# Weight halves of an MLP made by two Pool DMAs each, one casting and one adding

## The chip, the cores and the metric

The kernel runs on one core of one Trainium2 chip. The metric is the device time of one execution in microseconds (us); lower is better.

## The reference

The reference is one layer of a decoder trunk over 256 tokens of width 2048: RMSNorm, one combined projection into three attention mixers, three branch projections merged by sigmoid gates, an output projection with residual, and then the part that matters here, the MLP:

```python
h = rms_norm(x, norm_mlp[layer])
x = x + jnp.square(jax.nn.relu(h @ w_mlp_in[layer])) @ w_mlp_out[layer]
return rms_norm(x, norm_final)
```

`w_mlp_in` is 2048 x 8192 and `w_mlp_out` 8192 x 2048, both float32. The two are 134.2 MB together, and each weight is used once per execution.

## The kernel before, in words

Every dense product is done in three passes of a rounded format (`float32r`, F32R): a float32 number is split into a high part `hi` and a low part `lo = w - hi`, and the products hi x hi, hi x lo and lo x hi are summed in PSUM.

All dense work is one list, `steps`. A step is 512 KB of weights (128 partitions x 1024 numbers) and the matmuls that use them. For one step three things happen before TensorE can start: `load` (L67 to L70) fetches the raw weights with a DMA issued on SP, `fetch` (L72 to L81) makes `hi` as a copy with a change of type on ScalarE (L79) and `lo` as a subtraction on VectorE (L80). The tiles lie in the pool `ring`, with three tags (`raw`, `hi`, `lo`) of four buffers each.

The order of instructions on every engine is the order in which the code writes them (`manual_schedule`, L44). The last loop (L883 to L896) goes through the steps: it emits the preparation of a step (`pre`), one piece of the attention or transposition tasks (`advance`), what follows the step before (`post`, the emptying of PSUM), then `fetch` of the step `AHEAD` = 3 later, then the matmuls of the step itself.

The MLP is the last 256 steps. `mlp_in(p)` makes up to four groups of 256 hidden columns; each group is four steps of `dmajor` (weights stationary, L224 to L228; rows of 256 numbers). Its result is emptied by `half` (L690), `hu` (L691, L692) and `hid` (L693, L694). `mlp_out(p)` is up to sixteen steps of `tmajor` (activations stationary, L251 to L253; rows of 512 numbers), and its result is added to `acc` (L704). The order is `mlp_in(0)`, then `mlp_in(p)` and `mlp_out(p - 1)` in turn, and at the end `mlp_last`, whose four steps (L720 to L722) do the first token tile, then the second one from the same weights, then the last norm.

The Pool queue carries few things: small constants at the start, `spread_rows` (L195) and `load_master` (L203) for the attention bias, two memsets (L540), `load_nf` (L764, the gains of the last norm) and some arithmetic of the last norm. None of the weights go through it.

Of the kernel before, what the change touches and what calls it, by code (L numbers as in the profile page):

```python
# [8 lines left out]
F32 = mybir.dt.float32  # L9
F32R = mybir.dt.float32r  # L10
AF = mybir.ActivationFunctionType
OP = mybir.AluOpType
# [10 lines left out]
NB = 383  # L23
AHEAD = 3

# column offsets in w_in
AQ, AKC, AVC, AKS, AVS, AKW, AVW = 0, 1024, 1280, 1536, 1792, 2048, 2304
BQ, BK, BV = 2584, 3608, 3864
CQ, CK, CV = 4120, 5144, 5400
# [4 lines left out]
def hybrid_block(ctx: ExitStack, tc: tile.TileContext, x, w_in, cmp_pos, cmp_w1, cmp_w2, swa_sinks,  # L34
                 w_branch, w_out, w_mlp_in, w_mlp_out, norm_mix, norm_mlp, norm_final, rel_bias,
                 onehot, rmask, cmask, out):
    nc = tc.nc
    big = ctx.enter_context(tc.tile_pool(name="big", bufs=6))
    ring = ctx.enter_context(tc.tile_pool(name="ring", bufs=4))
# [15 lines left out]
    def pair(name="pair"):  # L55
        return psum.tile([128, 2, 512], F32, name=name, tag="mm")

    # ---------------------------------------------------------------- streamed weights
    steps = []
    tasks = []  # L60

    def add(src, a, b, mm, pre=None, post=None):
        steps.append((src, a, b, mm, pre, post))
# [3 lines left out]
    def load(j):  # L67
        src, a, b = steps[j][:3]
        loaded[j] = ring.tile([128, a, b], F32, name="raw", tag="raw")
        nc.sync.dma_start(loaded[j], src)  # L70

    def fetch(j):  # L72
        if j not in loaded:
            load(j)
        raw = loaded.pop(j)
        a, b = steps[j][1:3]
        hi = ring.tile([128, a, b], F32R, name="hi", tag="hi")
        lo = ring.tile([128, a, b], F32R, name="lo", tag="lo")
        nc.scalar.activation(hi, raw, AF.Copy)  # L79
        nc.vector.tensor_tensor(lo, raw, hi.bitcast(F32), op=OP.subtract)  # L80
        return hi, lo  # L81
# [10 lines left out]
        while any(t[0] == name for t in tasks):  # L92
            advance()

    # ---------------------------------------------------------------- constants
    xt = bigt([128, 2, D], F32, "xt")

    def load_x(c0, c1):
# [29 lines left out]
    hm = cst.tile([128, 4], F32, name="hm")  # L128
    nc.vector.tensor_reduce(hm, ident.rearrange("p (h c) -> p h c", h=4), axis=AX.X, op=OP.add)

    # ---------------------------------------------------------------- first norm
    part = cst.tile([128, 2, 4], F32, name="part")
    rs = cst.tile([128, 2], F32, name="rs")
    rsh = cst.tile([128, 2], F32, name="rsh")
# [2 lines left out]
    HT = [bigt([128, 8, 512], F32R, f"HT{i}") for i in range(2)]  # L137

    def split_scaled(tiles, k, src, g0):
        """hi and lo parts of two K tiles, src * gain, into columns 0:256 and 256:512."""  # L140
        d = [tiles[(k + a) // 8][:, (k + a) % 8] for a in range(2)]
        g = [gains[:, g0 + k + a:g0 + k + a + 1] for a in range(2)]
        for a in range(2):
            nc.scalar.activation(d[a][:, 0:256], src[:, a], AF.Copy, scale=g[a])
        for a in range(2):
            nc.vector.scalar_tensor_tensor(d[a][:, 256:512], src[:, a], g[a], d[a][:, 0:256].bitcast(F32),
                                           op0=OP.mult, op1=OP.subtract)
# [4 lines left out]
        nc.vector.tensor_copy(gains[:, c0:c0 + n], pc[:, 0:n])  # L152

    def x_block(i):
        """Two K tiles of x * gain; the row factor of the norm follows where products leave PSUM."""
        b = bank("xT").rearrange("p (a q) -> p a q", a=2)
        for a in range(2):
            k = 2 * i + a
            for tt in range(2):
                nc.tensor.transpose(b[:, a, tt * 128:(tt + 1) * 128], xt[:, tt, k * 128:(k + 1) * 128], ident)  # L160
        split_scaled(HT, 2 * i, b, 0)
# [29 lines left out]
        yield  # L191

    def spread_rows(m):
        """Row h 128 times at pitch 384; read at pitch 383 it is a Toeplitz matrix."""
        nc.gpsimd.dma_start(scr[m * 8:(m + 1) * 8, :, 0:NB],  # L195
                            rm[m * 8:(m + 1) * 8, None, :].to_broadcast([8, 128, NB]))

# [6 lines left out]
                                       ap=[[383, 128], [128 * 384, 4], [1, 256]]))  # L204
        masters[m, g] = t

    # ---------------------------------------------------------------- dense jobs
    def dmajor(w, c0, rhs, evac, kts=KT, pre=None, cuts=(0, 4, 8, 12, 16)):
        """256 columns of w as [column, token]: weights stationary."""
        st = {}  # L210
        for k0, k1 in zip(cuts, cuts[1:]):
            src = w[k0 * 128:k1 * 128, c0:c0 + 256].rearrange("(k p) c -> p k c", p=128)

            def mm(hi, lo, k0=k0, k1=k1):
                if k0 == 0:
                    st["ps"] = pair()
                ps = st["ps"]
                for k in range(k1 - k0):
                    kt = k0 + k
                    r = rhs(kt)  # L220
                    for c in range(2):
                        cs = slice(c * 128, (c + 1) * 128)
                        if kt:
                            nc.tensor.matmul(ps[:, c, 0:256], lo[:, k, cs], r[:, 0:256],  # L224
                                             start=False, stop=False)
                        nc.tensor.matmul(ps[:, c, :], hi[:, k, cs], r, start=kt == 0, stop=kt == kts - 1)  # L226
                        if not kt:
                            nc.tensor.matmul(ps[:, c, 0:256], lo[:, k, cs], r[:, 0:256],  # L228
                                             start=False, stop=False)

            add(src, k1 - k0, 256, mm, pre if k0 == 0 else None,
                (lambda: evac(st["ps"])) if k1 == kts else None)

    def tmajor(w, c0, n, lhs, evac, kts=KT, kc=2, pre=None):
        """n columns of w as [token, column]: activations stationary."""
        st = {}
        for k0 in range(0, kts, kc):
            src = w[k0 * 128:(k0 + kc) * 128, c0:c0 + n].rearrange("(k p) c -> p k c", p=128)

            def mm(hi, lo, k0=k0):  # L240
                if k0 == 0:
                    st["ps"] = pair()
                ps = st["ps"]
                for k in range(kc):
                    kt = k0 + k
                    l = lhs(kt)
                    for tt in range(2):
                        o = ps[:, tt, 0:n]
                        lh = l[:, tt * 128:(tt + 1) * 128]
                        ll = l[:, 256 + tt * 128:256 + (tt + 1) * 128]  # L250
                        nc.tensor.matmul(o, lh, hi[:, k], start=kt == 0, stop=False)  # L251
                        nc.tensor.matmul(o, lh, lo[:, k], start=False, stop=False)  # L252
                        nc.tensor.matmul(o, ll, hi[:, k], start=False, stop=kt == kts - 1)  # L253

            add(src, kc, n, mm, pre if k0 == 0 else None,
                (lambda: evac(st["ps"])) if k0 + kc == kts else None)
# [19 lines left out]
        for tt in range(2):  # L276
            nc.scalar.activation(dst[:, tt], ps[:, tt, c0:c0 + n], func, scale=scale[:, tt:tt + 1])

    # ---------------------------------------------------------------- projections
    w = w_in[0]  # L280
    qT, kT, vt = {}, {}, {}

# [36 lines left out]
            tasks.append(("A", attn_a(1)))  # L319
        tmajor(w, AVW, 280, hT, ev, kc=2)  # L320

    # ---------------------------------------------------------------- compression of blocks
    XH = {}
    kcT = cst.tile([128, 30], F32, name="kcT")
    vcr = cst.tile([128, 2, 128], F32, name="vcr")
# [86 lines left out]
            nc.vector.tensor_copy(vcr, pk[:, 0:256].rearrange("p (g d) -> p g d", g=2))  # L412
        yield

    # ---------------------------------------------------------------- attention
    oT = {}

    def new_o(m):
# [1 line left out]
            oT[m] = bigt([128, 8, 512], F32R, "oT")  # L420

    def core(m, g, q, k, v, o, first, last, gate):
        """Causal attention of the four heads of one kv group; o accumulates [d, (head, token)]."""
        M = masters[m, g]
        h0 = 4 * g
        qp = att.tile([128, 2, 4, 128], F32R, name="qp", tag="P0")
# [9 lines left out]
        for i in range(2):  # L436
            b = bank("s1").rearrange("p (h k) -> p h k", h=2)
# [143 lines left out]
        store_o(0, g, o)  # L581
        yield

    # ---------------------------------------------------------------- gates and branches
    gt = {}

    def gates(m):
# [26 lines left out]
            tmajor(w_branch[0, m], c * 512, 512, lambda kt: oT[m][:, kt], ev, kts=8, pre=pre)  # L614

    def to_dmajor(src, c, dst, gain0):
        """Column chunk c of a [token, column] tile, transposed and split into hi and lo parts."""
        if not dst:
            dst += [bigt([128, 8, 512], F32R, "dmaj") for _ in range(2)]
        for i in range(2):  # L620
# [12 lines left out]
                split_scaled(dst, k, b, gain0)  # L633
            yield

    # ---------------------------------------------------------------- output projection
    acc = {}
    H2 = []

# [34 lines left out]
        nc.vector.reciprocal(r2, r2)  # L674
        yield

    # ---------------------------------------------------------------- MLP
    hid = {}

    parts = [(4 * i, 4) for i in range(7)] + [(28, 3), (31, 1)]  # L680
# [27 lines left out]
    fin = {}  # L708

    def mlp_last(p):  # L710
        """The last K tiles: the first token tile is done before the second, from the same weights."""
        keep = []
        r0 = parts[p][0] * 256

# [68 lines left out]
            nc.scalar.dma_start(rows[:, 1280:2048], o[:, 1280:2048])  # L783
            nc.sync.dma_start(rows[:, 640:1280], o[:, 640:1280])

    # ---------------------------------------------------------------- order of the work
    def job(f, *a, **kw):
        """The steps of one dense job, taken off the list."""
        n = len(steps)
        f(*a, **kw)  # L790
        r = steps[n:]
        del steps[n:]
        return r
# [29 lines left out]
    n = len(steps)  # L823
# [28 lines left out]
    n = len(steps)  # L852
    out_proj()
    steps[n + 6] = before(steps[n + 6], lambda: drain("M"))
    n = len(steps)
    mlp_in(0)
    steps[n + 3] = before(steps[n + 3], lambda: drain("H"))
    for p in range(1, len(parts)):
# [3 lines left out]
    mlp_last(len(parts) - 1)  # L862
    steps[n - 4] = before(steps[n - 4], load_nf)

    # ---------------------------------------------------------------- emission
    ready = {}
    load_x(0, 256)
    load(0)
# [17 lines left out]
    for j in range(len(steps)):  # L886
        _, _, _, mm, pre, post = steps[j]
        if pre:
            pre()
        advance()  # L890
        if late:
            late()
        if j + AHEAD < len(steps):
            ready[j + AHEAD] = fetch(j + AHEAD)
        mm(*ready.pop(j))
        late = post  # L896

# [3 lines left out]


def _constants():
    """Distance buckets and causal masks of the two token tiles: they follow from the shapes alone."""
    import math
    import numpy as np
    dist = 255 - np.arange(NB)
# [28 lines left out]
```

## Time and profile before

| | |
|---|---|
| median of 2 runs | 1610.4 us (1610.1 to 1610.7) |
| profiled execution, span | 1610.1 us |
| TensorE busy | 1534.5 us, 95% |
| VectorE busy | 940.4 us, 58% |
| ScalarE busy | 718.8 us, 45% |
| Pool busy | 23.9 us, 1% |
| read from HBM | 290.02 MB |

The span is the time from the first to the last instruction of one profiled execution. Busy shares are means over stages that differ. The MLP is the stretch from about 889 us to the end, and what a change to it does is read there.

### The profile page before, as it was taken

The numbers are of one execution on the slowest core, as the hardware profiler recorded it, in microseconds if no ns is written. First come the engines' busy times: TensorE is split into PE (matmuls) and PEld (weight loads), VectorE is DVE, ScalarE is ACT, GpSimd is POOL, SyncE is SP. The second block draws the span as 40 slices with busy tenths as digits, with TensorE's granted clock in tenths as the row PEclk, the third lists the DMA queues.
The fourth block names the chain that finished last, engine by engine and source line by source line (L and its number), as shares of the span: only waits on it lengthen the run. The fifth ranks groups of instructions, "written<-read, shape, count | busy, mean of one in ns | idle before, by whom it ended". The sixth has DMA issues, their size and how long they took to land.

```text
span 1610.1 us, 20195 instructions
## 1 busy us (share of the span) xinstructions
PE 1534.5 (95%) x7878; PEld 1305.1 (81%) x7878; DVE 940.4 (58%) x1082; ACT 718.8 (45%) x942; POOL 23.9 (1%) x33
## 2 busy tenths in 40 slices
PE   8995997899959999999999999999999999999997
PEld 7894885688849888888888888888888888888885
DVE  5772663565637547744755666565655566555656
ACT  6551542455524445444445444343434444443443
POOL 1000000000000000000000000000000000000002
PEclk9997999899979999999999999999999999999999
DMA  8696756655666665566655656656565656566563
GB/s 248 193 276 110 223 158 126 174 169 173 176 138 172 183 194 187 168 183 192 225 187 184 188 177 197 192 190 190 186 195 188 193 181 198 181 198 194 189 218 118
DMA packets 211231, 298.16 MB, mean 185 GB/s; under 512 B 10268, under 2 KB 129612, under 8 KB 210752
## 3 DMA queue, kind: packets, MB, share of 16 engines
q1 hardware_dynamic: 207504, 287.15, 58.2%
q0 software_dynamic: 3456, 9.33, 3.8%
q8 instruction: 61, 1.00, 0.3%
q10 hardware_dynamic: 176, 0.40, 0.1%
q14 instruction: 34, 0.28, 0.1%
HBM read 290.02 MB, written 6.80 MB: 184 GB/s over the span
## 4 chain that ended last, share of the span: by engine, by line
PE 90%; DMA 7%; DVE 1%; issue 1%; ACT 1%; POOL 0%; POOLq 0%; DVEq 0%; ACTq 0%
PE pair L226 22%; PE pair L251 17%; PE pair L253 17%; PE pair L252 17%; PE pair L224 11%; DMA raw<-in_w_in_dram 5%; DMA raw<-in_w_branch_dram 2%; PE s L440 1%; PE obank L509 1%; PE pair L228 1%; DVE lo L80 1%; ACT hi L79 1%; PE tm L625 0%; PE obank L512 0%; PE cps L362 0%
## 5 line engine op out<-in xcount | busy, mean ns | idle before, releaser
L80 DVE TENSOR_TENSOR lo<-raw,hi 128x1024 fp32r<-128x1024 f32 (+2 forms) x542 | 653.5, 1213 | 540.1 <-ACT hi L79 538.9
L79 ACT ACTIVATE hi<-raw 128x1024 fp32r<-128x1024 f32 (+2 forms) x542 | 564.3, 1048 | 668.7 <-PE pair L253 385.5
L226 PE MATMUL pair<-dmaj,hi 128*128 128x512 f32 x1024 | 359.8, 398 | 0.0
L224 PE MATMUL pair<-dmaj,lo 128*128 128x256 f32 x960 | 269.7, 281 | 0.0
L226 PEld LDWEIGHTS pair<-dmaj,hi 128*128 128x128 f32 x1024 | 190.8, 188 | 44.5
L226 PE MATMUL pair<-HT,hi 128*128 128x512 f32 x576 | 206.8, 401 | 0.0
L251 PE MATMUL pair<-hi,hid 128*128 128x512 f32 x496 | 192.9, 389 | 0.0
L252 PE MATMUL pair<-lo,hid 128*128 128x512 f32 x496 | 192.9, 389 | 0.0
L253 PE MATMUL pair<-hi,hid 128*128 128x512 f32 x496 | 192.9, 389 | 0.0
L251 PE MATMUL pair<-hi,HT 128*128 128x512 f32 (+2 forms) x512 | 190.0, 371 | 2.7 <-ACT hi L79 2.7
L252 PE MATMUL pair<-lo,HT 128*128 128x512 f32 (+2 forms) x512 | 187.6, 366 | 0.4 <-DVE lo L80 0.4
L253 PE MATMUL pair<-hi,HT 128*128 128x512 f32 (+2 forms) x512 | 187.6, 366 | 0.0
L224 PEld LDWEIGHTS pair<-dmaj,lo 128*128 128x128 f32 x960 | 181.3, 189 | 1.4
L224 PE MATMUL pair<-HT,lo 128*128 128x256 f32 x540 | 153.1, 284 | 2.0 <-DVE lo L80 2.0
L226 PEld LDWEIGHTS pair<-HT,hi 128*128 128x128 f32 x576 | 109.4, 191 | 23.8 <-PE obank L576 0.2
L251 PEld LDWEIGHTS pair<-hi,HT 128*128 128x128 f32 x512 | 98.0, 191 | 17.6 <-ACT hi L79 3.0
L252 PEld LDWEIGHTS pair<-lo,HT 128*128 128x128 f32 x512 | 98.1, 192 | 15.3 <-DVE lo L80 0.6
L253 PEld LDWEIGHTS pair<-hi,HT 128*128 128x128 f32 x512 | 98.0, 191 | 15.3
L252 PEld LDWEIGHTS pair<-lo,hid 128*128 128x128 f32 x496 | 93.1, 188 | 19.4
L253 PEld LDWEIGHTS pair<-hi,hid 128*128 128x128 f32 x496 | 93.1, 188 | 19.4
L251 PEld LDWEIGHTS pair<-hi,hid 128*128 128x128 f32 x496 | 93.1, 188 | 18.9
L224 PEld LDWEIGHTS pair<-HT,lo 128*128 128x128 f32 x540 | 103.0, 191 | 3.1 <-DVE lo L80 2.2
(211 smaller groups left out, 1354.2 us busy)
## 6 DMA issues: line engine op xcount, KB each, us to landing
raw<-in_w_in_dram SPq DMA_DIRECT2D x178, 512.0 KB, 3.8
raw<-in_w_mlp_in_dram SPq DMA_DIRECT2D x128, 512.0 KB, 3.9
raw<-in_w_mlp_out_dram SPq DMA_DIRECT2D x128, 512.0 KB, 4.4
raw<-in_w_branch_dram SPq DMA_DIRECT2D x48, 512.0 KB, 4.4
raw<-in_w_out_dram SPq DMA_DIRECT2D x32, 512.0 KB, 4.4
raw<-in_cmp_w_dram SPq DMA_DIRECT2D x16, 512.0 KB, 4.6
scr<-rm POOLq DMA_DIRECT2D x3, 1532.0 KB, 36.1
master<-scr POOLq DMA_DIRECT2D x6, 512.0 KB, 5.2
```

What stands on the lines that cost most here:

```text
L79: nc.scalar.activation(hi, raw, AF.Copy)
L80: nc.vector.tensor_tensor(lo, raw, hi.bitcast(F32), op=OP.subtract)
L224: nc.tensor.matmul(ps[:, c, 0:256], lo[:, k, cs], r[:, 0:256], start=False, stop=False)
L226: nc.tensor.matmul(ps[:, c, :], hi[:, k, cs], r, start=kt == 0, stop=kt == kts - 1)
L228: nc.tensor.matmul(ps[:, c, 0:256], lo[:, k, cs], r[:, 0:256], start=False, stop=False)
L251: nc.tensor.matmul(o, lh, hi[:, k], start=kt == 0, stop=False)
L252: nc.tensor.matmul(o, lh, lo[:, k], start=False, stop=False)
L253: nc.tensor.matmul(o, ll, hi[:, k], start=False, stop=kt == kts - 1)
L440: nc.tensor.matmul(b[:, h], qp[:, a, 2 * i + h], kp[:, c], start=n == 0, stop=n == 2)
L509: nc.tensor.matmul(ob, v[:, a, 0, g * 128:(g + 1) * 128], P0[c][:, hs], start=first and n == 0, stop=False, skip_group_check=True)
```

## The change

For the steps of the MLP alone (index `from_dma[0]` and up) `fetch` no longer loads raw weights. One DMA on the Pool queue reads the weights into `hi`, a tile of type F32R; ScalarE writes `lo = -hi`; a second DMA on the Pool queue reads the same weights again and adds them onto `lo`. The twelve buffers of the ring are shared out so that each step takes two of them and six steps fit. The steps of the MLP are fetched five ahead in place of three. (The rest of the diff removes comments.)

```diff
+    from_dma = [1 << 30]
...
+    def fetch_by_dma(j):
+
+        src, a, b = steps[j][:3]
+        tags = ("raw", "hi", "lo")
+        hi = ring.tile([128, a, b], F32R, name="hi", tag=tags[2 * j % 3])
+        lo = ring.tile([128, a, b], F32R, name="lo", tag=tags[(2 * j + 1) % 3])
+        nc.gpsimd.dma_start(hi, src)
+        nc.scalar.activation(lo, hi.bitcast(F32), AF.Copy, scale=-1.0)
+        nc.gpsimd.dma_start(lo, src, accum_op=OP.add)
+        return hi, lo
+
     def fetch(j):
+        if j >= from_dma[0]:
+            return fetch_by_dma(j)
         if j not in loaded:
             load(j)
...
     n = len(steps)
+    from_dma[0] = n
     mlp_in(0)
...
-        if j + AHEAD < len(steps):
-            ready[j + AHEAD] = fetch(j + AHEAD)
+        for i in range(j + 1, min(j + (AHEAD if j < from_dma[0] else AHEAD + 2), len(steps) - 1) + 1):
+            if i not in ready:
+                ready[i] = fetch(i)
         mm(*ready.pop(j))
```

## Rows read from the trace of the kernel before

**Rows 1.** The page, busy time (us, share, instructions) and granted clock by slices.
```profile
PE 1534.5 (95%) x7878; PEld 1305.1 (81%) x7878; DVE 940.4 (58%) x1082; ACT 718.8 (45%) x942; POOL 23.9 (1%) x33
...
PEclk9997999899979999999999999999999999999999
```

**Rows 2.** Busy time by windows: stretch, length, engines, PEclk, DMA share, GB/s.
```profile
905.00:1560.00 655.00, 655.00 (x3327) 556.63 (x3326) 388.28 (x386) 282.30 (x300) 0.55 (x1) 1.00 0.61 191
```

**Rows 3.** The chain that ended last, MLP: start us, us, what.
```profile
1034.72 0.46 PE pair L226 x2
...
1123.39 0.46 PE pair L226 x2
```

**Rows 4.** Groups by line and form in 905:1560: busy us, mean ns, idle before.
```profile
L80 DVE TENSOR_TENSOR lo<-raw,hi 128x1024 fp32r<-128x1024 f32 x237 | 287.4, 1224 | 197.8 <-ACT hi L79 197.8
L79 ACT ACTIVATE hi<-raw 128x1024 fp32r<-128x1024 f32 x238 | 248.4, 1056 | 271.8 <-PE pair L253 162.2 <-PE pair L226 78.8 <-ACT hi L79 22.7
```

**Rows 5.** The page, DMA issues: count, KB each, median us to landing.
```profile
raw<-in_w_mlp_in_dram SPq DMA_DIRECT2D x128, 512.0 KB, 3.9
raw<-in_w_mlp_out_dram SPq DMA_DIRECT2D x128, 512.0 KB, 4.4
```

**Rows 6.** The timeline of POOL: start us, us, instruction, idle before.
```profile
163.37 0.78 POOL L203 DMA_DIRECT2D master<-scr  x1 [34.21 <-DMA raw<-in_w_in_dram]
164.14 0.33 POOL L540 MEMSET Lc<- 128x256 f32 x1
252.15 0.76 POOL L203 DMA_DIRECT2D master<-scr  x1 [87.67 <-DVE L L450]
...
1544.68 0.55 POOL L764 DMA_DIRECT2D nf<-in_norm_final_dram  x1 [924.56 <-DMA raw<-in_w_mlp_out_dram]
```

**Rows 7.** The timeline of PE around the wait of Rows 6.
```profile
157.30 1.03 PE L378 MATMUL cT<-fold,cs 60*128 60x30 f32 x4 [17.89 <-DVE cs L372]
```

**Rows 8.** The timeline of DVE ahead of the second `master` DMA.
```profile
251.17 0.68 DVE L450 SCALAR_TENSOR_TENSOR L<-s,master 128x512 f32<-128x512 f32 x1
251.77 1.21 DVE L454 TENSOR_REDUCE nm<-L 128x4 f32<-128x1024 f32 x1
```

**Rows 9.** The line L203: its Pool DMAs of 512 KB, us to landing.
```profile
DMA to landing us min/median/max: 4.2/5.2/6.4
```

**Rows 10.** The line L70 in 905:1560: SP's loads of 512 KB, us to landing.
```profile
DMA to landing us min/median/max: 3.4/4.0/5.9
```

**Rows 11.** DMA queues in 905:1560: packets, MB, share of 16 engines.
```profile
q1 hardware_dynamic: 94146, 123.75, 60.0%
```

**Rows 12.** DMA queues and issues in 128:164, where `scr` is written from Pool.
```profile
q0 software_dynamic: 704, 1.57, 43.1%
...
scr<-rm POOLq DMA_DIRECT2D x1, 1532.0 KB, 35.1
```

**Rows 13.** DMA queues and issues in 1544:1552, where `nf` is loaded.
```profile
q0 software_dynamic: 144, 1.05, 33.5%
...
nf<-in_norm_final_dram POOLq DMA_DIRECT2D x1, 1024.0 KB, 7.0
```

**Rows 14.** Busy time by windows (as Rows 2): the busiest DMA stretch, and two idle ones.
```profile
10.00:15.00 5.00, 5.00 (x29) 4.51 (x28) 2.34 (x5) 1.98 (x4) 0.00 (x0) 1.00 1.06 353
...
140.00:146.00 6.00, 0.00 (x0) 0.00 (x0) 0.00 (x0) 0.00 (x0) 0.00 (x0) 0.62 0.60 83
146.00:152.00 6.00, 0.00 (x0) 0.00 (x0) 0.00 (x0) 0.00 (x0) 0.00 (x0) 0.50 0.51 61
```

**Rows 15.** The timeline at the edges of the MLP, and the last step group.
```profile
873.52 27.78 SPq L70 DMA_DIRECT2D raw<-in_w_mlp_in_dram  x11
...
889.15 0.39 PE L226 MATMUL pair<-dmaj,hi 128*128 128x512 f32 x1
...
1588.15 0.39 PE L720 MATMUL pair<-hi,hid 128*128 128x512 f32 x1
```

## The prediction

> **What bounds the kernel now.** I read the page first: TensorE is busy 95% of the span, and its granted clock is low only in slices of the first third [rows 1]. Then the windows: from 905 to 1560 us, nearly the whole MLP, TensorE is busy 655.00 of 655.00 us at a granted clock of 1.00, and the DMA engines are at 0.61 with 191 GB/s [rows 2]. The chain of waits says the same: in the MLP it names only matmuls, and repeats after 1123.39 - 1034.72 = 88.67 us for 32 steps, **2.77 us a step** [rows 3]. The groups by line show the split: 1.06 us of ScalarE and 1.22 us of VectorE a step, both waiting for others [rows 4]. So nothing that the change removes ends anything last in this stage. What it puts in must stay below 2.77 us a step, or it becomes the bound.
>
> **What is removed.** 256 loads on SP [rows 5], 256 subtractions (256 x 1.22 = 313 us of VectorE) and 256 copies on ScalarE, which come back as 256 negations of the same size, 1.06 us [rows 4]. All of it lay beside the matmuls: worth nothing.
>
> **What is added: 512 DMAs on Pool, in a chain.** Pool's order per step is: DMA into hi, then DMA onto lo. The second waits for the negation, the negation for the landing of hi; and behind the waiting lo DMA stands the hi DMA of the next step. Does Pool hold what stands behind? At 163.37 it issues a DMA for which it had waited, and a memset follows at 164.14 [rows 6]. The memset's buffer had last been read by matmuls that end at 158.33 [rows 7], so it could have run some 5 us earlier: it was held. Fetching five steps ahead doesn't help, since the chain links each step to the next: hi(j), negation(j), lo(j), hi(j+1). One link costs:
>
> - From the end of the negation to lo's issue: 0.3 us, as from the end of the VectorE operation before L454 (251.85) to Pool's DMA at 252.15 [rows 6, 8]. Landing to negation isn't shown by itself; I count it in the landing.
> - Issue of lo: 0.76 us, as the Pool DMA of 512 KB in rows of 1 KB [rows 6]; 0.55 us, as for nf, at the low end [rows 6].
> - hi(j+1) from issue to landing: 4.2 us, the shortest of the six `master` DMAs of the same size [rows 9]. I take the shortest because the other traffic of the stage (SP's loads) is gone; the longest, 6.4, is the high end. The cast, which no row shows, is in this spread.
> - hi(j+1) behind lo(j): the two follow each other through the same 16 engines, hi's issue 0.76 us later. A plain load of 512 KB keeps all 16 busy 0.600 x 655 / 236 = 1.67 us (123.75 MB are 236 loads) [rows 11]. The add must also read what is there, twice the reads: I take 3.34 us, an estimate, so hi waits 3.34 - 0.76 = 2.58 us. Low end 0 (the two overlap; less is excluded, as lo's transfer can't speed hi's). High end: the one Pool write that was slow, 43.1% of 36 us = 15.5 us for 1.57 MB, so 5.2 us per 512 KB [rows 12], a wait of 4.44 us. I stay nearest to the plain row, since the weights' rows are long and contiguous.
> - The negation: 1.06 us [rows 4].
>
> The sum is 0.3 + 0.76 + 4.2 + 2.58 + 1.06 = **8.9 us a step**, against 2.77. Low end: 0.3 + 0.55 + 4.2 + 0 + 1.06 = 6.1. High end: 0.3 + 0.76 + 6.4 + 4.44 + 1.06 = 13.0.
>
> The doubled reads have a parallel in the Trainium skill ("Collectives: The Full Stack", section "The bandwidth ceiling: the fold count and why AG ≠ RS ≠ AR"): the DMA's add emits two reads per chunk, and the collective that adds moves half as much per second as the one that copies. No row here shows an adding DMA.
>
> **What hides under the chain.** TensorE's step takes 2.77 us, and 5.5 us if its clock falls to half, which rows with TensorE idle show: 0.50 from 146 to 152 us [rows 14]. Both are below 6.1, so TensorE only waits. PSUM is emptied behind the negation of a step four later on ScalarE's queue, but the matmuls that need that bank also need lo of that step, which comes after the same negation: no extra wait. half, hu and hid (some 2.7 us, once in four steps) then sit ahead of the next negation, in the time in which its hi is still on the way (4.2 us or more). If hi landed at once this cover would be gone, and they would cost up to 2.7 us in each of 32 groups, 86 us. nf (1.05 MB) moves past Pool's weight DMAs near the end: 0.55 us of issue and 33.5% of 8 us = 2.7 us of engines [rows 13], some 3 us. The ring's buffers bind nothing: hi(j+6) needs step j done.
>
> **The sum.** The first hi DMA can leave between SP's first MLP load now, 873.5, and about 881, three steps before the MLP's first matmul at 889.15 [rows 15]: 878. lo of that step is issued 4.2 + 1.06 + 0.3 later, at 883.6; lo of the last step 255 links later, 883.6 + 255 x 8.9 = 3153. It lands after 4.2 + 1.67 = 5.9. After the last step's weights come its matmuls and the last norm. Now these take from 1588.15 + 3 x 1.36 = 1592.2 to 1610.1 = 17.9 us [rows 15]; 30 matmuls of 0.227 us at half clock add 6.8. With nf: 3153 + 5.9 + 24.7 + 3 = 3187, **3190 us**. The profiled execution (1610.1) and the median (1610.4) are the same here. Ends: 883.6 + 255 x 6.1 + 4.2 + 17.9 = 2460; 883.6 + 255 x 13.0 + 8 + 27.7 = 4230.
>
> **Rivals.**
>
> - *Pool doesn't hold hi(j+1)*, steps overlap, and the DMA engines bind: 1.67 + 3.34 = 5.0 us a step, 878 + 256 x 5.0 + 30 = 2190 us; with an add as cheap as a copy 3.34, 1765 us. For it: twelve buffers and five steps of look-ahead. Against: the held memset. 0.07.
> - *Short DMAs*: hi lands in 3.4 us, the shortest of SP's loads [rows 10], and isn't delayed by lo: 0.3 + 0.55 + 3.4 + 1.06 = 5.3, 883.6 + 255 x 5.3 + 3.4 + 17.9 = 2256 us. Against: none of six Pool DMAs landed below 4.2. 0.04. The Trainium skill ("DMA: Bandwidth & Descriptors", section "Anatomy of one DMA — SWDGE (gpsimd) path") has a rule for this: about 2.0 us plus the bytes at 436 GB/s, 3.2 us for 512 KB; with that the link would be 0.3 + 0.76 + 3.2 + 0.44 + 1.06 = 5.8 and the time about 2385. By that rule, the trace doesn't agree: its Pool DMAs took 1.0 to 3.2 us longer [rows 9].
> - *The add is far slower* than any row: four times the scr rate, 20.8 us, a link of 26 us and some 7600 us. For it: no row shows an add. 0.04.
> - *Not slower*: both DMAs of every step are done within 2.77 us and TensorE stays without gaps, so 1610 us. That needs 1.05 MB in 2.77 us = 379 GB/s with nothing for the add's second read; the best 5 us here are 353, with the engines full [rows 14]. It decides only if the chain doesn't. 0.015. Faster by over 2% is 32 us, and the stage has no idle TensorE time to give: 0.005.
> - *The change doesn't do what it says*: if the DMA into hi copied the bits without rounding, lo would come out zero; the same DMAs and waits remain, and so the time.
>
> **How the numbers follow.** The serial chain between 6.1 and 13.0 us a link has 0.83; the rivals take the rest. The range, 2460 to 4230, is that case alone and leaves out 0.17. A measurement of this kernel can tell about 2% from no change. Slower by over 2%: 0.98; within: 0.015; faster: 0.005.
>
> **What would show it.** Right: Pool's waits split between ScalarE (negation) and nothing else; the chain of waits in the MLP made of DMA hi, ACT, POOL; the MLP's DMA issue rows showing hi at 4 to 7 us to landing and the start of consecutive lo issues 8.9 us apart; granted clock near 0.5; TensorE's idle time put down to the DMA onto lo. HBM reads up by 134 MB to about 424 MB. Wrong: hi issues of several steps in a row with no lo between (Pool passes), a gap between lo issues under 6 or over 13 us, or DMA share near 1 (the engines bind, not the chain). The term I trust least is the add: if hi's landing is much beyond 4.2 + 2.6 us, that is the one that was mis-sized.

## The result, and the profile after

The changed kernel takes **3233.6 us** (3232.3 to 3234.8, 2 runs) against 1610.4: a ratio of 2.008, 95% interval 2.004 to 2.012. The forecast was 3190 us in a range of 2460 to 4230. The profiled execution has a span of 3230.5 us, and its terms are taken against that.

The page after: busy time, and by slices of 1/40 of the span TensorE's busy tenths, its granted clock and the share of the DMA engines; then the Pool queue's packets and the memory traffic.

```profile
PE 2100.9 (65%) x7878; PEld 1666.3 (52%) x7878; DVE 631.2 (20%) x826; ACT 721.3 (22%) x942; POOL 527.0 (16%) x545
...
PE   9797989999955555555555555555555555555554
...
PEclk9898989999966766666666667666666666666776
DMA  7766566666566655565566556555655655555555
...
q0 software_dynamic: 208256, 277.80, 44.2%
...
HBM read 424.24 MB, written 6.80 MB: 133 GB/s over the span
```

The first eleven slices, to 888 us, are the part ahead of the MLP's matmuls, which the change doesn't touch; from the MLP on, TensorE is busy half the time. The memory is read for 134 MB more, the second read of the MLP's weights. And yet the DMA engines' share is no higher than before (0.59 here against 0.61 [rows 2]), and no engine is full. That points to latencies that follow one another. The windows of the MLP (length, PE, PEld, DVE, ACT, POOL busy, granted clock, DMA share, GB/s) say the same:

```profile
905.00:3180.00 2275.00, 1249.06 (x3505) 944.18 (x3505) 112.98 (x167) 301.29 (x318) 492.23 (x501) 0.69 0.59 116
```

The waits of the whole execution (engine and line, what it waited for, us in total, times, longest):

```profile
POOL lo L81 <- ACT lo L80: 1779.2, 250, 8.9
...
ACT lo L80 <- DMA hi<-in_w_mlp_out_dram: 987.0, 128, 10.4
ACT lo L80 <- DMA hi<-in_w_mlp_in_dram: 984.7, 128, 8.8
...
PEld pair L266 <- DMA lo<-in_w_mlp_out_dram: 556.4, 123, 6.2
PE pair L266 <- DMA lo<-in_w_mlp_out_dram: 491.9, 123, 5.8
```

Pool waits for the negation, the negation for hi's landing, TensorE for lo's. That is the chain of the prediction, read from the waits. The page's own chain of waits doesn't show it: it has 59% under "issue", time for which it found no releaser, so it can't serve as the evidence here.

The start of the MLP shows the chain link by link. The timeline of ScalarE and Pool (start us, us, instruction, idle before and its releaser; the other engines' rows are left out):

```profile
877.63 0.75 POOL L79 DMA_DIRECT2D hi<-in_w_mlp_in_dram  x1 [261.16 <-PE pair L267]
...
881.89 1.06 ACT L80 ACTIVATE lo<-hi 128x1024 fp32r<-128x1024 f32 x1 [5.95 <-DMA hi<-in_w_mlp_in_dram]
...
883.25 1.33 POOL L81 DMA_DIRECT2D lo<-in_w_mlp_in_dram  x1 [4.88 <-ACT lo L80]
...
884.04 1.32 POOL L79 DMA_DIRECT2D hi<-in_w_mlp_in_dram  x1
...
891.12 1.06 ACT L80 ACTIVATE lo<-hi 128x1024 fp32r<-128x1024 f32 x1 [8.17 <-DMA hi<-in_w_mlp_in_dram]
...
892.48 1.27 POOL L81 DMA_DIRECT2D lo<-in_w_mlp_in_dram  x1 [7.12 <-ACT lo L80]
```

The first hi, with nothing of Pool's ahead of it, has its negation begin after 881.89 - 877.63 = 4.26 us. The second, issued 0.79 us behind a lo, takes 891.12 - 884.04 = 7.08. From one lo to the next it is 9.23 us: 0.79 to hi's issue, 7.08, 1.06, and 0.30 back to Pool. A link of 8.95 us, by the same view further on:

```profile
1513.34 1.19 POOL L81 DMA_DIRECT2D lo<-in_w_mlp_out_dram  x1 [7.06 <-ACT lo L80]
...
1514.07 1.17 POOL L79 DMA_DIRECT2D hi<-in_w_mlp_out_dram  x1
...
1520.94 1.06 ACT L80 ACTIVATE lo<-hi 128x1024 fp32r<-128x1024 f32 x1 [7.90 <-DMA hi<-in_w_mlp_out_dram]
...
1522.29 1.19 POOL L81 DMA_DIRECT2D lo<-in_w_mlp_out_dram  x1 [7.05 <-ACT lo L80]
```

The last lo leaves at 3204.50, so 255 links took 3204.50 - 883.25 = 2321 us, **9.10 us a link** on average. The page's DMA issues (count, KB each, median us to landing) give the landings that belong to it; SP's loads of the same weights took 3.9 and 4.4 [rows 5]:

```profile
hi<-in_w_mlp_in_dram POOLq DMA_DIRECT2D x128, 512.0 KB, 6.8
lo<-in_w_mlp_in_dram POOLq DMA_DIRECT2D x128, 512.0 KB, 6.2
hi<-in_w_mlp_out_dram POOLq DMA_DIRECT2D x128, 512.0 KB, 6.9
lo<-in_w_mlp_out_dram POOLq DMA_DIRECT2D x128, 512.0 KB, 6.2
```

### The profile page after: what moved, and what is told of

Read it like the earlier page. It is cut to its first block, busy times and chain, and to the rows that moved or that the text cites. A ratio compares the mean times of both kernels' runs of the same rounds, so it can differ in the third digit from the quotient of the medians.

```text
span 3230.5 us, 20274 instructions
## 1 busy us (share of the span) xinstructions
PE 2100.9 (65%) x7878; PEld 1666.3 (52%) x7878; DVE 631.2 (20%) x826; ACT 721.3 (22%) x942; POOL 527.0 (16%) x545
## 4 chain that ended last, share of the span: by engine, by line
issue 59%; PE 23%; POOL 14%; DMA 3%; DVE 1%; ACT 0%; POOLq 0%; DVEq 0%; ACTq 0%
POOL hi L79 9%; PE pair L265 5%; PE pair L267 5%; PE pair L266 5%; POOL lo L81 4%; PE pair L240 4%; DMA raw<-in_w_in_dram 2%; PE pair L238 2%; DMA raw<-in_w_branch_dram 1%; PE s L454 0%; PE obank L523 0%; DVE lo L94 0%; PE cps L376 0%; PE cps L375 0%; ACT hi L93 0%
## 5 line engine op out<-in xcount | busy, mean ns | idle before, releaser
L80 ACT ACTIVATE lo<-hi 128x1024 fp32r<-128x1024 f32 x256 | 270.5, 1057 | 1971.8 <-DMA hi<-in_w_mlp_out_dram 987.0
L238 PE MATMUL pair<-dmaj,lo 128*128 128x256 f32 x960 | 391.0, 407 | 412.9 <-DMA lo<-in_w_mlp_in_dram 390.1
L266 PE MATMUL pair<-lo,hid 128*128 128x512 f32 x496 | 314.0, 633 | 491.9 <-DMA lo<-in_w_mlp_out_dram 491.9
L240 PE MATMUL pair<-dmaj,hi 128*128 128x512 f32 x1024 | 578.4, 576 | 0.6 <-DVE dmaj L160 0.6
L94 DVE TENSOR_TENSOR lo<-raw,hi 128x1024 fp32r<-128x1024 f32 (+2 forms) x286 | 343.2, 1203 | 324.2 <-ACT hi L93 323.0
L93 ACT ACTIVATE hi<-raw 128x1024 fp32r<-128x1024 f32 (+2 forms) x286 | 297.0, 1041 | 370.4 <-PE pair L267 200.8
L81 POOL DMA_DIRECT2D lo<-in_w_mlp_in_dram x128 | 163.0, 1274 | 907.6 <-ACT lo L80 885.4
L81 POOL DMA_DIRECT2D lo<-in_w_mlp_out_dram x128 | 152.5, 1192 | 916.3 <-ACT lo L80 893.8
L265 PE MATMUL pair<-hi,hid 128*128 128x512 f32 x496 | 284.0, 573 | 8.0 <-DVE hu L705 8.0
L267 PE MATMUL pair<-hi,hid 128*128 128x512 f32 x496 | 288.5, 582 | 0.0
L79 POOL DMA_DIRECT2D hi<-in_w_mlp_in_dram x128 | 160.3, 1252 | 261.2 <-PE pair L267 261.2
```

Source lines behind the costliest of these rows:

```text
L79: nc.gpsimd.dma_start(hi, src)
L80: nc.scalar.activation(lo, hi.bitcast(F32), AF.Copy, scale=-1.0)
L81: nc.gpsimd.dma_start(lo, src, accum_op=OP.add)
```

## The experiments

The theory: each step is a link of one chain, because Pool's queue holds the next hi DMA behind the lo DMA that waits; the link's length is issue, hi's landing behind lo's transfer, negation. The rivals: the DMA engines are the bound already; the casting DMA is slow by itself; the look-ahead is what matters. Every kernel was run once, beside the kernel before (1608.9 to 1611.7 us). All edits are to the changed kernel; `...` marks lines left out. All kernels but two (the copy and the small add in the chain) also look ahead three steps in place of five, and so the look-ahead comes first.

**Look-ahead of three steps.**

```diff
-        for i in range(j + 1, min(j + (AHEAD if j < from_dma[0] else AHEAD + 2), len(steps) - 1) + 1):
+        for i in range(j + 1, min(j + (AHEAD if j < from_dma[0] else AHEAD), len(steps) - 1) + 1):
```

> The changed kernel with three steps of look-ahead in the MLP, as before, in place of five. If the steps are links of one chain, the number in flight does not matter: 3230 us, within 20. If the look-ahead carries part of the latency (steps overlap), fewer in flight make it slower, up to 5/3 of the MLP's time: between 3300 and 4700 us.

Measured: 3218.8 us, 15 us (0.5%) less. The number of steps fetched ahead does next to nothing: they aren't in flight together.

**hi issued two steps ahead of lo.** The ring and the DMAs are the same; Pool's order differs, and the look-ahead is the three steps of the kernel just seen.

```diff
+    def early_hi(j):
+        src, a, b = steps[j][:3]
+        early[j] = ring.tile([128, a, b], F32R, name="hi", tag=("raw", "hi", "lo")[2 * j % 3])
+        nc.gpsimd.dma_start(early[j], src)
...
-        hi = ring.tile([128, a, b], F32R, name="hi", tag=tags[2 * j % 3])
+        for i in range(j, min(j + 2, len(steps) - 1) + 1):
+            if i not in early:
+                early_hi(i)
+        hi = early[j]
...
-        nc.gpsimd.dma_start(hi, src)
         nc.scalar.activation(lo, hi.bitcast(F32), AF.Copy, scale=-1.0)
         nc.gpsimd.dma_start(lo, src, accum_op=OP.add)
```

> The same two DMAs for each MLP step, but Pool issues the hi DMA two steps ahead of the lo DMA, so that the hi of the next steps no longer stand behind a lo that waits. (lo is made three steps ahead in place of five, as the ring has twelve buffers.) If Pool's order is what makes the chain, the DMA engines become the bound, at the 5.3 us a step that they are busy now (0.586 of 9.07 us): about 890 + 256 x 5.3 + 25 = 2270 us, with a DMA share near 1. If the engines or the memory bind already, or the look-ahead does not matter, it stays at about 3230 us. Not below 2.77 us a step and 1610 us in any case.

Measured: 1915.7 us. The order on Pool was worth 1318 us of the 1623 us lost; as the look-ahead is worth nothing, that settles the cause. But 1915.7 is far from the 2270 expected: a step took 3.9 us, not 5.3. In a window of its MLP (columns as above) the DMA share is beyond 1:

```profile
1000.00:1500.00 500.00, 388.81 (x1781) 293.57 (x1779) 55.78 (x80) 153.05 (x160) 251.78 (x256) 1.00 1.24 267
```

The queue's row for the same window (packets, MB, share of 16 engines) gives the step: 133.37 MB of 1.0486 MB each in 500 us are 127 steps, 3.93 us each.

```profile
q0 software_dynamic: 101535, 133.37, 124.2%
```

So the packets' times overlap within an engine, and a busy share worked out under light load, 0.586 of 9.07 us, is no measure of what the engines can carry.

**hi issued three steps ahead.** The same with `j + 3` in place of `j + 2`; it asks whether 3.9 us is the engines' limit or a longer loop of latencies.

> Both full DMAs of each MLP step, with the hi DMA issued three steps ahead of the lo DMA in place of two. With two ahead a step took 3.9 us, and hi landed 9.4 us after its issue. If the DMA engines' throughput is the bound there, the time stays at 1915 us within 15 and hi's landing grows by a step, to some 13 us. If three steps in a loop of latencies (landing, negation, issue) are the bound, a fourth shortens the step to about 3.9 x 3 / 4 = 2.9 us and the time to about 1670 us.

Measured: 1924.2 us. hi's landing grew from 9.4 to 11.9 us by the median, while the memory brought 266 GB/s, as with two steps (267): more DMAs queue, none is done sooner. So with both halves by Pool the transfers are taken to be the limit at 3.9 us a step, above TensorE's 2.77. The test isn't quite clean: Pool's hi DMAs wait for free buffers for 280 of the 500 us, so the fourth hi is only partly in flight, and the landing stays under the 13 us expected. The landing rows of hi's DMAs from 1000 to 1500 us, two steps ahead and three:

```profile
DMA to landing us min/median/max: 8.5/9.4/11.3
...
DMA to landing us min/median/max: 8.7/11.9/13.3
```

**A copy in place of the add, in the chain.**

```diff
-        nc.gpsimd.dma_start(lo, src, accum_op=OP.add)
+        nc.gpsimd.dma_start(lo, src)
```

> The second Pool DMA of each MLP step copies the weights onto lo instead of adding them (lo is then the weights themselves: the subtraction is left out). Every wait and issue of the chain stays. If hi waits behind lo's transfer and the add costs that transfer a second read, the link of 9.05 us falls by one plain load, 1.67 us, to some 7.4 us and the time to about 2810 us. If an add costs the DMA engines no more than a copy, nothing changes: about 3230 us. If hi's 6.8 us come from the cast or from the stage and not from what is ahead of it, nothing changes either, and hi still lands after 6.8 us.

Measured: 2788.1 us, 445 us less, 1.75 us a link. hi lands after 4.9 and 5.3 us in place of 6.8 and 6.9, as the page's DMA issues have it:

```profile
hi<-in_w_mlp_in_dram POOLq DMA_DIRECT2D x128, 512.0 KB, 4.9
lo<-in_w_mlp_in_dram POOLq DMA_DIRECT2D x128, 512.0 KB, 4.2
hi<-in_w_mlp_out_dram POOLq DMA_DIRECT2D x128, 512.0 KB, 5.3
lo<-in_w_mlp_out_dram POOLq DMA_DIRECT2D x128, 512.0 KB, 4.4
```

The add costs the DMA that stands behind it 1.75 us more than a copy does, close to the 1.67 us of one plain load that the prediction put in for the second read. But not all of it need be transfer. Pool's own instruction is longer for an adding DMA, and so is the one for the hi behind it. The groups on Pool (count, busy us, mean ns), of the changed kernel and then of this one:

```profile
L81 POOL DMA_DIRECT2D lo<-in_w_mlp_out_dram x128 | 152.5, 1192 | 916.3 <-ACT lo L80 893.8 <-ACT half L704 22.5
L79 POOL DMA_DIRECT2D hi<-in_w_mlp_out_dram x128 | 150.4, 1175 | 0.0
...
L79 POOL DMA_DIRECT2D hi<-in_w_mlp_out_dram x128 | 90.3, 705 | 1.0 <-PE pair L267 1.0
L81 POOL DMA_DIRECT2D lo<-in_w_mlp_out_dram x128 | 89.4, 698 | 778.8 <-ACT lo L80 771.5 <-ACT half L704 7.3
```

hi's instruction starts some 0.73 us behind lo's in both and ends 0.5 us later with the add, about when a second instruction of 0.7 us would that starts when lo's has ended. If hi's transfer waits for that end, some 0.5 of the 1.75 us is Pool's issue and 1.2 the add's transfer. No run separates the two.

**A small add.** Only 64 of 1024 numbers a partition are added.

```diff
-        nc.gpsimd.dma_start(lo, src, accum_op=OP.add)
+        nc.gpsimd.dma_start(lo[:, 0:1, 0:64], src[:, 0:1, 0:64], accum_op=OP.add)
```

> The second Pool DMA of each MLP step adds only 64 of the 1024 numbers of each partition (the low half is left unfinished). Its place in Pool's order, and its wait for the negation, stay. If the chain is serial and hi's landing is 4.2 us alone plus what it waits behind lo, the link is 0.3 + 0.6 + 4.2 + 1.06 = 6.2 us and the time about 884 + 255 x 6.2 + 25 = 2490 us, with hi landing after some 4.2 us. If hi's transfer is slow by itself in this stage, hi still takes 6.8 us, the link is 8.8 and the time about 3150 us. If nothing is serial and the engines' traffic binds, the halved traffic gives 2.77 us a step and 1610 us.

Measured: 2551.6 us, 62 above the expectation. With little ahead of it, the casting DMA lands about as the first one of the changed kernel did (the page's DMA issues):

```profile
hi<-in_w_mlp_in_dram POOLq DMA_DIRECT2D x128, 512.0 KB, 4.4
hi<-in_w_mlp_out_dram POOLq DMA_DIRECT2D x128, 512.0 KB, 4.2
```

The links on Pool's timeline are 6.4 us apart, with one of 7.1 here:

```profile
1407.31 0.85 POOL L81 DMA_DIRECT2D lo<-in_w_mlp_in_dram  x1 [4.77 <-ACT lo L80]
1407.87 1.04 POOL L79 DMA_DIRECT2D hi<-in_w_mlp_in_dram  x1
1413.75 0.85 POOL L81 DMA_DIRECT2D lo<-in_w_mlp_in_dram  x1 [4.83 <-ACT lo L80]
1414.93 0.76 POOL L79 DMA_DIRECT2D hi<-in_w_mlp_in_dram  x1 [0.33 <-issue]
1420.81 0.84 POOL L81 DMA_DIRECT2D lo<-in_w_mlp_in_dram  x1 [5.13 <-ACT lo L80]
```

The excess is nearly all hi's way from issue to negation, 4.44 us by the median in place of 4.2. The rest is links like the last one, in which hi leaves 0.6 us late and waits for nothing that the profile shows: 16 of 256. What that is stays open.

**A plain first DMA, and the small add.** ScalarE makes hi from the raw tile.

```diff
+        raw = ring.tile([128, a, b], F32, name="raw", tag="raw")
...
-        nc.gpsimd.dma_start(hi, src)
...
+        nc.gpsimd.dma_start(raw, src)
+        nc.scalar.activation(hi, raw, AF.Copy)
         nc.scalar.activation(lo, hi.bitcast(F32), AF.Copy, scale=-1.0)
-        nc.gpsimd.dma_start(lo, src, accum_op=OP.add)
+        nc.gpsimd.dma_start(lo[:, 0:1, 0:64], src[:, 0:1, 0:64], accum_op=OP.add)
```

> The chain with the small second DMA (64 of 1024 numbers of each partition; the low half is left unfinished), but the first Pool DMA is a plain load into a raw tile, and ScalarE makes hi from it and then lo = -hi: one ScalarE operation of 1.06 us more in each link, and no cast in the DMA. If the cast costs the transfer nothing, the link is 1.06 us longer than with the cast and the small second DMA, 7.3 in place of 6.2 us: about 2760 us, with the landing at the same 4.2 us. If the cast doubles the transfer's 1.67 us, the landing is 1.67 us shorter than with the cast and the time about 2330 us.

Measured: 2805.6 us, 254 above the small add with the cast: 1.00 us a link, against 1.06 for the extra ScalarE operation. The cast has no price that shows in this chain; the landings are the same:

```profile
raw<-in_w_mlp_in_dram POOLq DMA_DIRECT2D x128, 512.0 KB, 4.4
raw<-in_w_mlp_out_dram POOLq DMA_DIRECT2D x128, 512.0 KB, 4.1
```

**Only hi by a Pool DMA.** SP loads the raw weights, Pool loads hi, VectorE subtracts.

```diff
+        if j not in loaded:
+            load(j)
+        raw = loaded.pop(j)
...
         nc.gpsimd.dma_start(hi, src)
-        nc.scalar.activation(lo, hi.bitcast(F32), AF.Copy, scale=-1.0)
-        nc.gpsimd.dma_start(lo, src, accum_op=OP.add)
+        nc.vector.tensor_tensor(lo, raw, hi.bitcast(F32), op=OP.subtract)
```

> Only the hi half by a Pool DMA: SP loads the raw weights as before, Pool loads the same weights into hi with the cast, and VectorE makes lo = raw - hi. No instruction on Pool waits for another engine except for free buffers. If a casting DMA costs what a plain load does, the engines are asked for 2 x 1.67 = 3.34 us a step: 890 + 256 x 3.34 + 25 = 1770 us, with a DMA share near 1. If the cast costs double, 1.67 + 3.34 = 5.0 us a step and 2200 us. If the second copy of the weights is nearly free, 2.77 us a step and 1610 us.

Measured: 1692.1 us, 83 us above the kernel before and 78 under the expectation. There is no chain through Pool's queue left, and every weight is still read twice: TensorE is busy 471 of 500 us while the DMAs bring 345 GB/s. hi lands after 6.8 and 6.9 us and raw after 6.5 and 6.7, where raw alone took 3.9 and 4.4 [rows 5]; that these longer landings make TensorE's gaps is argued, not shown.

```profile
1000.00:1500.00 500.00, 471.25 (x2289) 382.13 (x2288) 267.05 (x267) 24.60 (x40) 118.92 (x165) 1.00 1.24 345
```

**Only lo by a Pool DMA.** SP loads raw, ScalarE makes hi and -hi, Pool adds.

```diff
+        if j not in loaded:
+            load(j)
+        raw = loaded.pop(j)
...
-        nc.gpsimd.dma_start(hi, src)
...
+        nc.scalar.activation(hi, raw, AF.Copy)
         nc.scalar.activation(lo, hi.bitcast(F32), AF.Copy, scale=-1.0)
         nc.gpsimd.dma_start(lo, src, accum_op=OP.add)
```

> Only the lo half by a Pool DMA: the weights are loaded by SP as before, ScalarE makes hi and then lo = -hi, and Pool adds the weights onto lo. Pool's order holds one DMA a step and its wait does not hang on a Pool DMA. If the chain hi, negation, lo, hi was the bound, it is gone and the DMA engines bind: 5.3 us a step less what the cast costs over a plain load, 1.67 + 3.34 = 5.0 to 5.3, so 2200 to 2280 us. If an add is slow by itself (6.2 us each, one after the other), 6.2 to 6.5 us a step, about 2500 to 2580 us. If the add costs no more than a copy, 3.34 us a step and 1770 us.

Measured: 2037.8 us, none of the three expectations: 4.5 us a step. The chain no longer binds, as the theory says, but 4.5 lies above the 3.9 us of Pool's two DMAs, and the memory brings 235 GB/s here against 267 there:

```profile
1000.00:1500.00 500.00, 370.26 (x1583) 291.30 (x1582) 49.46 (x71) 251.20 (x254) 136.27 (x112) 0.90 1.08 235
```

What sets the 4.5 us stays open. One loop comes near it: lo lands 10.4 to 11.4 us after its issue, and the ring has four buffers of lo; landing, ScalarE's two operations and the matmuls over four buffers give about that period, (10.9 + 2.1 + 0.3 + 2.8 to 5.5) / 4 = 4.0 to 4.7. That is argued, not shown.

**hi issued two steps ahead, and a copy in place of the add.**

The edits of the two kernels together, at two steps ahead.

> As with hi issued two steps ahead of lo, but the second DMA copies the weights onto lo instead of adding them (the subtraction is left out). If the add's second read is what loads the engines, the step falls from 3.9 us to what two loads took with SP and Pool side by side, 3.04 us, so about 1690 us. If the add costs the engines nothing and only its latency counts, the step stays near 3.9 us and the time near 1915 us.

Measured: 1698.3 us, as with SP and Pool side by side (1692.1). With the add 1915.7: so with hi issued ahead, the add costs (1915.7 - 1698.3) / 256 = **0.85 us** a step more than a copy. In the chain it was 1.75.

```profile
1000.00:1500.00 500.00, 472.69 (x2276) 377.04 (x2275) 71.16 (x102) 195.28 (x203) 235.16 (x327) 1.00 1.38 341
```

That 0.85 is a difference of two kernels, and a price of the add in transfer only if transfers limit both. For the copying one this isn't shown. Its chain of waits (start us, us, what) runs from one hi over the negation and lo's issue to the hi of three steps later:

```profile
1200.47 7.30 DMA hi<-in_w_mlp_out_dram
...
1209.99 6.02 DMA hi<-in_w_mlp_out_dram
```

By the medians that loop is 6.8 + 0.1 + 1.06 + 0.3 + 0.7 = 9.0 us for three steps, 3.0 us each, against 3.08 measured (170.17 MB in the 500 us). If the transfers could go faster than that, the add costs them more than 0.85 us a step.

## Why the prediction was right

**The bound.** Nothing removed was on the path: the work of VectorE fell from 940.4 to 631.2 us, and it bought nothing. With neither the chain nor the add, two reads of each weight still end 83 and 87 us above the kernel before (1692.1 and 1698.3): the stage had no idle TensorE time to give, as the windows said [rows 2].

**The chain.** Pool holds what stands behind a waiting DMA. The memset held for 5 us [rows 6, 7] was the only sign of it before, and it was enough: the order is worth 1318 us, and the look-ahead nothing.

**The link.** Predicted 0.3 + 0.76 + 4.2 + 2.58 + 1.06 = 8.9. The link shown at 1513.34 is 0.29 + 0.73 + 6.87 + 1.06 = 8.95; the medians over all 256 steps are 0.30 + 0.76 + 6.94 + 1.06 = 9.06, and the mean link is 9.10. The two terms with bounds came out near the values taken. hi alone: 4.2 from the shortest `master` landing [rows 9]; measured 4.26 to the negation at the start and 4.2 to 4.4 behind the small add. The wait behind lo: 2.58 predicted; by the medians of the landings 6.85 - 4.3 = 2.5 measured, made of 0.8 for a copy (5.1 - 4.3) and 1.75 more for the add. The size is right, but the reason for it, that the add holds the engines for a second plain load, is not shown: some 0.5 us of the 1.75 may be Pool's longer issue, for which the prediction had no term. That 2.58 was met within 0.1 us, in bounds of 0 to 4.44, is in part luck. For the add the Trainium skill ("Collectives: The Full Stack", section "The bandwidth ceiling: the fold count and why AG ≠ RS ≠ AR") gives a reason, found on collectives: two source reads per chunk. By that rule the chain's 1.75 us, against 1.67 for one plain load, agrees in size; the 0.85 us with hi issued ahead neither agrees nor speaks against it, since it is only the least that the add costs there.

**The sum.** First lo at 883.25 (883.6 predicted), 255 links of 9.10 (8.9: 52 us more), then 26.0 us to the end (33.6 predicted: nf's 3 us fell into a link, and from the landing of the last lo it was 19.8 us in place of 24.7). Together 3230.5 against 3187. Of the link's 0.2 us, 0.16 is the way from hi's issue to the negation by the medians (6.94 against 4.2 + 2.58 = 6.78), in which the step from landing to negation, counted in the landing, is some 0.1; the other 0.04 is that the mean lies above the median, with nf's link of 11.4 us the longest. The length of the rows made little: the links of `w_mlp_in` average 9.14 us, those of `w_mlp_out` 9.06.

**What of it was wrong.** The first rival's price, 5.0 us a step if the engines bound, or 2190 us: it took busy time under light load for capacity. With hi issued ahead a step took 3.9, and the time is 1915.7. It changed nothing here, since the case didn't come, but that number would have misled anybody who fixed the order next. The page's chain of waits, named as what would show the steps, showed "issue". And the granted clock was foreseen near 0.5 and was 0.69. From 1510.7 us on, after idling for 4.1 us, TensorE did twelve matmuls at 0.50 (1.2 GHz), most of them 0.63 us long; in the twelve from 1519.6 on, after 3.4 us idle, it went from there to 1.00 (2.4 GHz) and 0.40 us.

**The short-DMA rival** needed a landing of 3.4 us for hi, without delay by lo. Its page's rule, 2.0 us plus the bytes at 436 GB/s (the Trainium skill, "DMA: Bandwidth & Descriptors", section "Anatomy of one DMA — SWDGE (gpsimd) path"), gives an estimate of 3.2 us for 512 KB. By that rule the runs with a nearly empty queue don't agree: from the start of the issue they gave 4.1 to 4.4, cast or not, of which Pool's instruction is 1.0 (985 to 1016 ns).

## What to carry to other kernels

Where one queue issues both a DMA and the DMA that needs its result, fetching further ahead doesn't overlap the steps: write out the queue's order, find the wait, and name what stands behind it. Issuing the independent DMA two steps ahead of the waiting one broke the chain here (3233.6 to 1915.7 us). But in a stage that TensorE fills, work taken from other engines is worth nothing, and the kernels that read the weights twice without the chain and the add were still 83 and 87 us slower than before.

## What the runs showed of the hardware

- An adding DMA of 512 KB costs 1.75 us more than a copy for the DMA behind it when the queue is nearly empty. With hi issued two steps ahead the difference is 0.85 us a step, the least that it can be where transfers limit.
- Pool's instruction for an adding DMA of 512 KB took 1.18 to 1.29 us, where two follow each other and where it stands alone (only lo by Pool); for a copying or casting one it took 0.70 to 0.75 us, unless it stood behind an adding one.
- The cast from float32 to float32r changed the landing by nothing that shows (4.2 to 4.4 us against 4.1 to 4.4), but it takes more packets: with the small add behind it the Pool queue moved 142720 packets in the whole run, with the plain load in its place 77184, which is 256 fewer for each of the 256 loads.
- The busy share of the DMA engines went to 1.24 and 1.38 over 500 us: it isn't bounded by 1. At 0.59 it had foretold 5.3 us a step, and 3.9 was measured: it isn't a share of capacity.
